# Four head groups and a memory attention: projections in another order, the gates of two groups in one product, 46 products ahead of the inverses

## The chip, the core and the metric

The kernel runs on one core of a Trainium2 chip. The metric is the device time of one execution in microseconds (us); the median of 3 runs of the kernel before is 945.6 us (944.08 to 947.56).

The engines are named as in the profile: PE (TensorE, the matrix engine; PEld is its weight load), DVE (VectorE), ACT (ScalarE), POOL (GpSimd) and SP (SyncE, which here only issues transfers). Each engine works through its own list of instructions in order and waits for others by semaphores.

## What is computed

One layer on `x` of 1024 tokens by 1024 features, in float32. All four head groups read one normalised input through one combined projection:

```python
h = rms_norm(x, pre_norm_g)
proj = h @ w_in + b_in      # columns: a_q a_k a_v a_i a_f a_z | b_x b_z | c_r c_k c_v c_w c_a c_z | d_q d_k d_v d_f d_z
h_a = mlstm_chunkwise(a_q, a_k, a_v, a_i, a_f)     # A: matrix memory in chunks, stabilised by a running maximum
h_b = multiscale_pool(b_x)                         # B: trailing means over 2, 4, 8, 16
h_c = rwkv7_time_mix(c_r, c_k, c_v, c_w, c_a)      # C: S = S(diag(w) - kk^T (a kk)) + v^T k, step by step
h_d = forgetting_attention(d_q, d_k, d_v, d_f)     # D: softmax(q k^T/8 + F_t - F_s), F = cumsum log sigmoid(d_f)
y = concat(h_a*silu(a_z), h_b*silu(b_z), h_c*silu(c_z), h_d*silu(d_z)) @ w_out
x = x + rms_norm(y, post_norm_g)
x = x + rms_norm(memory_cross_attention(rms_norm(x), mem), xattn_post_g)   # 256 memory tokens, 4 heads
```

Group C is computed in 16 chunks of 64 tokens. Each chunk and head has a 64x64 triangular system, whose inverse is put together from 32x32 blocks. Group D is FoX, group A the mLSTM.

## The kernel before

**Products in three parts.** A float32 product is made of three passes: each operand is split into a high and a low part (`h` and `l` of the input, `wh` and `wl` of the weights), and `mm3` (lines 136 to 139) issues high by high, low by high and high by low. `wload` (line 111) loads a weight piece (`wr`), rounds it to `wh` on ACT (L122) and takes the rest `wl` on POOL (L126), or on DVE (L124) late in the program.

**Fillers.** The projections aren't run as one block. They are generators in a list, `fillers`, and `fill(n)` draws n units from it. A unit is three matmuls of 512 columns, or six of about 260 columns. The order of PE's instructions is the order of the code. The other engines' instructions are put in order by a planner, which orders by readiness and priority, so that what the code writes late may come early.

**The stages**, with their times in the profiled execution:

- to 150 us: input norm, transposes, projections of C (`cproj`, `cnorm`).
- 150 to 208: four `cprep`, which prepare decay, gates and the chunk operands of C (line 518 on). Behind each stands `fill(15)`. Among these fillers is the product of D's values and gates, `vgemm(O_DV, 260, 8, dvd)`: 256 columns of values and 4 gate columns, 32 units.
- 208 to 223: the "gram" products of C (L575). Their results are masked on POOL (L585, 16 of 64x512) and stored by SP to a scratch tensor `dN` (L592).
- `cinv` (line 595) inverts the 32x32 blocks: it loads `dN` into `n` (L597), prepares an identity on POOL (L599, L600), and runs 62 dependent operations on DVE (L604 and L606 in turn). The result goes out to `dTn` (L609) and `dTt` (L608), and `tinv(0)` loads 32x32 blocks of it (L618). Its first products are PE's L630, the next L638. `fill(NI)` with `NI = 70` stands between `cinv` and L630. Its units come from `rgemm(O_DK)` and `vgemm(O_AV, 264)` (A's values with 8 gate columns). The norm products of D's keys stand among them (L822, L823: sums of squares by a matrix of ones, whose inputs DVE splits in L161).
- 297 to 420: the chain of C over its chunks (`cprop`, L679 to L711), with `rgemm(O_AK)` and `zgemm(O_CZ, 2)` as fillers. `zgemm(O_CZ)` makes C's gate path: 96 matmuls of 512 columns.
- 434 to 529: the mLSTM over 8 tiles. `mpre` loads `e` (L1048, from `cd`), adds a mask on DVE (L1049), takes the exponential (L1051) and multiplies by the scores `ml` (L1055 on PE, L1057 on DVE). `mlstm` ends with a norm whose root is taken on POOL as a power (L143, L144), and `post()` scales by it (`hh`, L1087 on DVE, L1088 on POOL). The fillers around a tile are `G0, G1, GA, GB, GC = 14, 7, 2, 4, 4` (before the first, before the second, and three per tile), from `bgemm`, `zgemm(O_BZ)` and `zgemm(O_AZ)`. `post()` of tile i runs in tile i+1, that of the last behind the loop.
- from 538: FoX. `Fp` holds F per head and key, in two halves (`t<-fd`, L1196 loads), and POOL adds the causal mask to it (L1206, 8 of 128x256 for each half). Each step has PE's scores (L1254, L1255), DVE's sum (L1256), ACT's exponential (L1262, tile `lg`) and PE's transposes (L1272).
- to the end: output projection, memory attention.

Of the kernel before, what the change touches and what calls it, by code (L numbers as in the profile page):

```python
# [11 lines left out]
ALU = mybir.AluOpType  # L12
# [14 lines left out]
O_BX, O_BZ = 1032, 1288  # L27
# [4 lines left out]
def bcast(ap, n):  # L32
    return bass.AP(tensor=ap.tensor, offset=ap.offset, ap=[[0, 128], [1, n]])
# [3 lines left out]
def tile_trunk(ctx: ExitStack, tc: tile.TileContext, a, out, dbg=None):  # L37
# [73 lines left out]
    def wload(src, scale=None):  # L111
        shape = [src.shape[0], src.shape[1], src.shape[2]] if len(src.shape) == 3 else [src.shape[0], src.shape[1]]
        with tc.high_priority():
            raw = wtile("wr", shape)
            SY.dma_start(raw, src)
            hi, lo = wtile("wh", shape), wtile("wl", shape)
            if scale is not None:
                for x, c in enumerate(scale):
                    SC.activation(hi[:, x, :], raw[:, x, :], AF.Copy, scale=c)
                    V.scalar_tensor_tensor(lo[:, x, :], raw[:, x, :], c, f32(hi[:, x, :]), op0=ALU.mult, op1=ALU.subtract)  # L120
                return hi, lo
            SC.copy(hi, raw)  # L122
            if cur["wp0"] is not None:
                V.tensor_tensor(lo, raw, f32(hi), op=ALU.subtract)  # L124
            else:
                G.tensor_tensor(lo, raw, f32(hi), op=ALU.subtract)  # L126
        return hi, lo
# [13 lines left out]
    def rstd_pow(tag, ss, n, eps, w=1):  # L141
        r = base(tag, [128, w])
        G.tensor_scalar(r, ss, 1.0 / n, eps, op0=ALU.mult, op1=ALU.add)  # L143
        G.tensor_tensor(r, r, mhalf[:, 0:w], op=ALU.pow)  # L144
        return r

    def norm_rows(src, gbc, dst):
        r = base("tn", [128, 1])
        SC.activation(dst, src, AF.Square, accum_out=r)
        r = rstd_pow("tn", r, D, EPS)  # L150
        V.scalar_tensor_tensor(dst, src, r, gbc, op0=ALU.mult, op1=ALU.mult)

    def gload(pool, tag, ap):
# [84 lines left out]
    def xnorm(i):  # L238
        x_t = xp("x", [128, 1024])
        SY.dma_start(x_t, a["x"][0, i * 128:(i + 1) * 128, :])  # L240
        xn = xp("xn", [128, 1024])
        r = base("tn", [128, 1])
        SC.activation(xn, x_t, AF.Square, accum_out=r)
        r = rstd_pow("tn", r, D, EPS)
        V.tensor_scalar(xn, x_t, r, None, op0=ALU.mult)
        xn_.append(xn)

# [346 lines left out]

    def cinv():
        Nt = cc("n4", [128, 32, 32])
        SY.dma_start(Nt, dN)  # L597
        Tn = cc("n4", [128, 32, 32])
        G.memset(Tn, 0.0)  # L599
        G.memset(Tn.rearrange("p a b -> p (a b)")[:, ::33], 1.0)  # L600
        for j in range(31):
            m = 31 - j
            pr = cc("pr", [128, m, j + 1])
            V.tensor_tensor(pr, Nt[:, j, j + 1:32][:, :, None].to_broadcast([128, m, j + 1]),  # L604
                            Tn[:, j, 0:j + 1][:, None, :].to_broadcast([128, m, j + 1]), op=ALU.mult)
            V.tensor_tensor(Tn[:, j + 1:32, 0:j + 1], Tn[:, j + 1:32, 0:j + 1], pr, op=ALU.add)  # L606
        V.tensor_copy(Nt, Tn.rearrange("p a b -> p b a"))
        SY.dma_start(dTt, Nt)  # L608
        SY.dma_start(dTn, Tn)  # L609
# [45 lines left out]
            SC.copy(SV[c - 1][0:64, 1::2, :], p[0:64, :, 64:128])  # L655

    FA, FB, FC = 2, 2, 2
    NI = 70
    BN = {}

    def cbk(c):
# [81 lines left out]
            SY.dma_start(yu[i * 128:(i + 1) * 128, 1, :], yc)  # L743


    def vgemm(c0, n, gc0, dst):
        ng = n - 256
        b = cm("bias", [128, 264])
        SY.dma_start(b[:, 0:n], bcast(b_in[c0:c0 + n], n))

        zz = []

        def ev(i, p):
            if i % 2 == 0:
                zz.append(cur["stg"]("zu", [128, 2, 256]))
            z, g = zz[-1][:, i % 2, :], gates[:, i, gc0:gc0 + ng]
            SC.copy(z, p[:, 0:256])
            SC.copy(g, p[:, 256:n])  # L758
            if i % 2:
                V.tensor_tensor(zz[-1], zz[-1], b[:, None, 0:256].to_broadcast([128, 2, 256]), op=ALU.add)  # L760
                g = gates[:, i - 1:i + 1, gc0:gc0 + ng]
                V.tensor_tensor(g, g, b[:, None, 256:n].to_broadcast([128, 2, ng]), op=ALU.add)
                SY.dma_start(dst[(i - 1) * 128:(i + 1) * 128, :].rearrange("(a p) c -> p a c", a=2), zz[-1])
        yield from ngemm_q(w_in, c0, n, hact, ev)

    def zgemm(c0, g, halves=False):
        def ev1(c, hf, p):
# [183 lines left out]
    with tc.manual_schedule(engines={PE}):  # L951
        run(cproj(6, 1))
        run(cproj(2, 2))
        fillers += [cproj(0, 2), cproj(4, 2), vgemm(O_DV, 260, 8, dvd), rgemm(O_DQ, 66, 0, 46, (7, 5, 5, 5))]
        gs = [cnorm(hf, j) for hf in range(2) for j in range(2)]
        for g in gs:
            next(g)
# [8 lines left out]
        for n, g in enumerate(gs):  # L966
            with tc.issue_after(act["cnorm"].ins):
                next(g)
            if g is gs[-1]:
                act["ln"] = tc.keep_in_program_order(SC.preload_act_table_set("natural_log_exp_and_others"))  # L970
            fill(15)
            if n:
                run(gs[n - 1])
        fill(4)
        run(gs[-1])
        c1.close()
        fillers += [rgemm(O_DK, 68, 256, 47, (6, 6, 5, 5)), vgemm(O_AV, 264, 0, avd), rgemm(O_AQ, 0, 512)]
# [25 lines left out]
        for c in range(16):  # L1003
            cchain(c)
            if c < 3:
                next(ti[1], None)
            if c >= 3:
                next(gr, None)
            if c >= 9:
                next(ac, None)  # L1010
        run(ac)
        cstore()
# [47 lines left out]
    def mlstm(i, vt, e):  # L1060
# [6 lines left out]
        if i > 0:  # L1067
# [6 lines left out]
        dn = base("tm", [128, 4])  # L1074
# [7 lines left out]
        ss = base("tm", [128, 4])  # L1082
        V.tensor_reduce(ss, h4(sq), AX.X, ALU.add)
        r = rstd_pow("tm", ss, 64, EPS, 4)

        def post():
            V.tensor_tensor(h4(hh), h4(hh), bc4(r), op=ALU.mult)  # L1087
# [71 lines left out]
            V.tensor_tensor(hi[r2], raw[r2], f32(hi[r2]), op=ALU.subtract)  # L1159
            qst[h] = hi  # L1160

    fillers += [bgemm(), zgemm(O_BZ, 1), zgemm(O_AZ, 0)]
    G0, G1, GA, GB, GC = 14, 7, 2, 4, 4
    bp = [bpool(0), bpool(1)]
    with tc.manual_schedule(engines={PE}):
        fill(G0)
        pre = mpre(0)
        fill(G1)
        post = None
        for i in range(NT):  # L1170
# [29 lines left out]
    am.close()  # L1200
    db = Pool("db", {"v": 2, "lg": 2, "pt": 3, "rE": 1})
    V.tensor_scalar(maskD, maskD, -NEG, None, op0=ALU.mult)
    for i in range(NT):
        for j in range(2):
            t = Fp[j][:, :, i * 128:(i + 1) * 128]
            G.tensor_tensor(t, t, maskD[:, None, :].to_broadcast([128, 2, 128]), op=ALU.add)  # L1206
# [330 lines left out]
    for g in range(1, 3):  # L1537
# [51 lines left out]
```

## Time and profile before

| | |
|---|---|
| median of 3 runs | 945.6 us (944.08 to 947.56) |
| profiled execution | 945.55 us |
| its span on the core | 943.7 us |
| PE busy | 895.3 us, 6041 matmuls |
| DVE, ACT, POOL busy | 544.3, 440.0, 223.2 us |
| mean granted clock of PE | 0.988 |

The profiled execution is the one from which all durations come; it lies at the median of the runs. The span is 1.85 us shorter than the time of the same execution. In a row of the timeline the columns are start (us), duration (us), engine, line, operation, output<-inputs, shape, count, and in brackets the idle time of the engine just before with what ended it. A matmul's duration overlaps that of the next, so its price is the distance from one start to the next. PEclk is the granted clock as a share of full speed.

### The profile page before, as it was taken

How to read it: one execution, taken by the hardware profiler on the slowest of the kernel's cores; microseconds unless marked ns; L12 is line 12 of the kernel's file. 1: busy time of each engine (PE TensorE's matmuls, PEld its weight loads, DVE VectorE, ACT ScalarE, POOL GpSimd, SP SyncE). 2: the span in 40 equal slices, each digit the busy share in tenths (PEclk: the TensorE clock that was granted, in tenths of full speed). 3: DMA queues.
4: the chain of work that ended last, by engine and by line, in shares of the span. 5: the costliest groups of instructions: out<-in, count | busy, mean ns of one | idle time of the engine just before them, and what ended most of it. 6: DMA issues, size and time to landing. Idle time of an engine off the chain costs nothing. (4 is left out here: it accounts for less than half of the span.)

```text
span 943.7 us, 16237 instructions
## 1 busy us (share of the span) xinstructions
PE 895.3 (95%) x6041; PEld 757.4 (80%) x6041; DVE 544.3 (58%) x1265; ACT 440.0 (47%) x1009; POOL 223.2 (24%) x244
## 2 busy tenths in 40 slices
PE   6999999999799999998998979999999999999997
PEld 6988887887598777776776667888887888889997
DVE  7684046973873347662698547656675455554225
ACT  7587156545455345642443335444454343444221
POOL 1002221139212243533334622000000000121211
PEclk9999999999999999999999989999999999999999
DMA  8977211132244122316465667533245311153104
GB/s 281 287 226 247 80 45 46 34 85 35 90 139 110 39 87 78 124 46 157 119 172 150 212 204 227 175 93 101 79 146 205 96 34 35 34 177 111 38 1 179
DMA packets 94431, 113.86 MB, mean 121 GB/s; under 512 B 21072, under 2 KB 68752, under 8 KB 94352
## 3 DMA queue, kind: packets, MB, share of 16 engines
q1 hardware_dynamic: 94208, 112.71, 38.9%
q8 instruction: 48, 0.79, 0.3%
q14 instruction: 31, 0.25, 0.1%
q10 hardware_dynamic: 144, 0.11, 0.1%
HBM read 83.92 MB, written 28.87 MB: 120 GB/s over the span
## 5 line engine op out<-in xcount | busy, mean ns | idle before, releaser
L137 PE MATMUL mm<-h,wh 128*128 128x512 f32 x528 | 221.3, 419 | 0.3 <-ACT zu L773 0.3
L138 PE MATMUL mm<-l,wh 128*128 128x512 f32 x528 | 210.4, 399 | 0.0
L139 PE MATMUL mm<-h,wl 128*128 128x512 f32 x528 | 210.3, 398 | 0.0
L126 POOL TENSOR_TENSOR wl<-wr,wh 128x512 fp32r<-128x512 f32 (+2 forms) x74 | 101.6, 1375 | 372.6 <-ACT wh L122 356.4
L137 PEld LDWEIGHTS mm<-h,wh 128*128 128x128 f32 x528 | 101.2, 192 | 24.0 <-issue 1.1
L139 PEld LDWEIGHTS mm<-h,wl 128*128 128x128 f32 x528 | 101.0, 191 | 23.4
L138 PEld LDWEIGHTS mm<-l,wh 128*128 128x128 f32 x528 | 101.5, 192 | 17.3 <-issue 0.2
L122 ACT CAST wh<-wr 128x512 fp32r<-128x512 f32 (+2 forms) x122 | 74.6, 620 | 71.6 <-PE mm L138 32.5
L137 PE MATMUL mm<-wh,act 128*128 128x256 f32 x256 | 72.7, 284 | 0.0
L138 PE MATMUL mm<-wl,act 128*128 128x256 f32 x256 | 71.9, 281 | 0.0
L139 PE MATMUL mm<-wh,act 128*128 128x256 f32 x256 | 71.8, 281 | 0.0
L137 PE MATMUL mm<-h,act 128*128 128x512 f32 x128 | 53.6, 419 | 0.9 <-DVE zu L771 0.4
L139 PE MATMUL mm<-h,act 128*128 128x512 f32 x128 | 50.5, 394 | 0.0
L138 PE MATMUL mm<-l,act 128*128 128x512 f32 x128 | 50.2, 392 | 0.0
L137 PEld LDWEIGHTS mm<-wh,act 128*128 128x128 f32 x256 | 48.3, 189 | 0.1
L138 PEld LDWEIGHTS mm<-wl,act 128*128 128x128 f32 x256 | 48.3, 188 | 0.0
L139 PEld LDWEIGHTS mm<-wh,act 128*128 128x128 f32 x256 | 48.2, 188 | 0.0
L137 PE MATMUL mm<-mT,wh 128*128 128x256 f32 x128 | 37.3, 291 | 8.9 <-ACT wh L122 8.9
L137 PE MATMUL mm<-wh,h 128*128 128x260 f32 (+1 forms) x128 | 37.4, 292 | 2.5 <-ACT gates L758 1.6
L1519 DVE TENSOR_TENSOR o<-mm,gb 128x256 f32<-128x256 f32 x32 | 13.6, 424 | 43.8 <-ACT junk L1518 43.6
L1465 ACT ACTIVATE e<-lgp,tf,r 128x256 f32<-128x256 f32 x32 | 18.0, 564 | 43.2 <-DVE tf L1462 43.2
L139 PE MATMUL mm<-mT,wl 128*128 128x256 f32 x128 | 37.0, 289 | 0.3 <-DVE wl L124 0.3
(408 smaller groups left out, 1996.0 us busy)
## 6 DMA issues: line engine op xcount, KB each, us to landing
wr<-in_w_in_dram SPq DMA_DIRECT2D x50, 256.0 KB, 2.9
wr<-in_wkv_dram SPq DMA_DIRECT2D x32, 256.0 KB, 3.9
x<-in_x_dram SPq DMA_DIRECT2D x16, 512.0 KB, 5.1
x<-x1d SPq DMA_DIRECT2D x15, 512.0 KB, 5.7
wr<-in_xattn_wo_dram SPq DMA_DIRECT2D x16, 256.0 KB, 3.0
vwd<-row SPq DMA_DIRECT2D x8, 512.0 KB, 4.0
rT<-zu SPq DMA_DIRECT2D x16, 256.0 KB, 2.1
zT<-zu SPq DMA_DIRECT2D x16, 256.0 KB, 3.1
```

What stands on the lines that cost most here:

```text
L122: SC.copy(hi, raw)
L126: G.tensor_tensor(lo, raw, f32(hi), op=ALU.subtract)
L137: T.matmul(o, lh, rh, start=st, stop=False, skip_group_check=skip)
L138: T.matmul(o, lh, rl, start=False, stop=False, skip_group_check=skip)
L139: T.matmul(o, ll, rh, start=False, stop=sp, skip_group_check=skip)
L1465: SC.activation(e, p, AF.Exp, bias=nb, scale=r2[:, i:i + 1], accum_out=dn)
L1519: V.tensor_tensor(o3[i][:, gs], p, xog[:, gs], op=ALU.mult)
```

## The change

It moves projections and waits; the number of PE's matmuls stays the same.

- D's values leave the fillers of the `cprep` stage, without the gate columns (256 wide), and take the place of `zgemm(O_CZ)` in the chain of C. `zgemm(O_CZ)` goes behind the fillers of the mLSTM, where `G0, G1, GA, GB, GC` become 18, 9, 3, 5, 5.
- The four gate columns of D join A's values in one product of 268 columns, from an array `w_av` packed on the host. The gates of both groups are then copied at once.
- `fill(15)` becomes `fill(13)`, four times; `NI` goes from 70 to 46.
- The load of `dN` in `cinv` is issued by ACT and not by SP. A flag `vsplit` sends the low parts of weights from POOL to DVE between the last `cprep` and `cinv`.
- `post()` of the last mLSTM tile goes into the loop, ahead of its `fill(GC)`. In FoX the masks are written in `fmask(i)`, called one tile ahead. The convolution of A is drawn from chunk 8 on, not 9, and small tiles share one tag.

```diff
-            SY.dma_start(Nt, dN)       # cinv
+            SC.dma_start(Nt, dN)
...
-            if cur["wp0"] is not None:
+            if cur["wp0"] is not None or cur.get("vsplit"):
                 V.tensor_tensor(lo, raw, f32(hi), op=ALU.subtract)
...
-    NI = 70
+    NI = 46
...
-    def vgemm(c0, n, gc0, dst):
+    def vgemm(wd, bias, c0, n, dst):
...
-            z, g = zz[-1][:, i % 2, :], gates[:, i, gc0:gc0 + ng]
+            z = zz[-1][:, i % 2, :]
             SC.copy(z, p[:, 0:256])
-            SC.copy(g, p[:, 256:n])
+            if ng:
+                SC.copy(gates[:, i, :], p[:, 256:n])
...
-        fillers += [cproj(0, 2), cproj(4, 2), vgemm(O_DV, 260, 8, dvd), rgemm(O_DQ, 66, 0, 46, (7, 5, 5, 5))]
+        fillers += [cproj(0, 2), cproj(4, 2), rgemm(O_DQ, 66, 0, 46, (7, 6, 6, 6))]
...
-            fill(15)
+            fill(13)
             if n:
                 run(gs[n - 1])
+        cur["vsplit"] = True
         fill(4)
...
-        fillers += [rgemm(O_DK, 68, 256, 47, (6, 6, 5, 5)), vgemm(O_AV, 264, 0, avd), rgemm(O_AQ, 0, 512)]
+        fillers += [rgemm(O_DK, 68, 256, 47, (6, 6, 5, 5)), vgemm(a["w_av"], a["b_av"][0], 0, 268, avd), rgemm(O_AQ, 0, 512)]
...
         next(ti[0])
+        cur["vsplit"] = False
         fill(NI)
...
-        fillers += [rgemm(O_AK, 2, 768), zgemm(O_CZ, 2)]
+        fillers += [rgemm(O_AK, 2, 768), vgemm(w_in, b_in, O_DV, 256, dvd)]
...
-    fillers += [bgemm(), zgemm(O_BZ, 1), zgemm(O_AZ, 0)]
-    G0, G1, GA, GB, GC = 14, 7, 2, 4, 4
+    fillers += [bgemm(), zgemm(O_BZ, 1), zgemm(O_AZ, 0), zgemm(O_CZ, 2)]
+    G0, G1, GA, GB, GC = 18, 9, 3, 5, 5
...
             post = mlstm(i, *pre)
+            if i == NT - 1:
+                post()
             fill(GC)
...
-        post()
         next(bp[1])
...
-    for i in range(NT):
+    def fmask(i):
         for j in range(2):
             t = Fp[j][:, :, i * 128:(i + 1) * 128]
             G.tensor_tensor(t, t, maskD[:, None, :].to_broadcast([128, 2, 128]), op=ALU.add)
+
+    fmask(0)
...
+            if h == 1 and i < NT - 1:
+                fmask(i + 1)
```

Three places show what becomes of the order on the engines. Numbers at the names are those of the buffers; lines from 658 on are shifted by 2 to 8 in the kernel after.

The first is the load of `dN` ahead of the inverses. Before, it is the last of these rows on SP, behind a weight load `wr` that can only start when its buffer is free:

```order
L592 DMA dN<-bq_2296 32x8x32 x6
L592 DMA dN<-bq_2387 32x8x32 x8
L115 DMA wr_2827<-in_w_in_dram 128x2x256
L597 DMA n_439_2472<-dN 128x1024
L115 DMA wr_2879<-in_w_in_dram 128x2x264
L115 DMA wr_2897<-in_w_in_dram 128x2x264
```

After, it stands on ACT, between two steps of the norm of D's keys (`sm`, `zt`):

```order
L122 CAST wh_2623<-wr_2621 128x536
L828 ACTIVATE sm_2440<-sm_2440,epst 128x512
L809 ACTIVATE zt_2488<-zu_2195 128x512
L829 ACTIVATE sm_2440<-sm_2440 128x512
L597 DMA n_436_2326<-dN 128x1024
L160 CAST bv_2490<-zt_2488 128x256
```

The load has left the queue of weight loads; what POOL does ahead of the identity (L599) has not changed but for one low part.

The second is the start of the mLSTM on DVE (`e`: the tile of exponents, `q`: the low part of a convolved tile). Before, the product of the first tile stands behind the first mask:

```order
L1049 TENSOR_TENSOR e_4874<-e_4874,maskA 128x512
L1057 SCALAR_TENSOR_TENSOR e_4874<-ml_4881,e_4874 128x2x128
L1057 SCALAR_TENSOR_TENSOR e_4874<-ml_4882,e_4874 128x2x128
L1049 TENSOR_TENSOR e_4917<-e_4917,maskA 128x512
L1049 TENSOR_TENSOR e_5007<-e_5007,maskA 128x512
L1159 TENSOR_TENSOR q_5003<-u_5000,q_5003 64x1024
```

After, three masks stand ahead of it:

```order
L1053 TENSOR_TENSOR e_4732<-e_4732,maskA 128x512
L1053 TENSOR_TENSOR e_4781<-e_4781,maskA 128x512
L1053 TENSOR_TENSOR e_4890<-e_4890,maskA 128x512
L1061 SCALAR_TENSOR_TENSOR e_4732<-ml_4739,e_4732 128x2x128
L1061 SCALAR_TENSOR_TENSOR e_4732<-ml_4740,e_4732 128x2x128
L1061 SCALAR_TENSOR_TENSOR e_4781<-ml_4788,e_4781 128x2x128
```

The first product now needs the loads of three tiles of `e`, not of one.

The third is the start of FoX on POOL (`t`: the two halves of `Fp`; `tm` and `tc`: the root of the last mLSTM tile). Before:

```order
L126 TENSOR_TENSOR wl_5926<-wr_5923,wh_5925 128x512
L1206 TENSOR_TENSOR t_5808<-t_5808,maskD 128x2x128 x8
L126 TENSOR_TENSOR wl_5953<-wr_5950,wh_5952 128x512
L1206 TENSOR_TENSOR t_5811<-t_5811,maskD 128x2x128 x8
L143 TENSOR_SCALAR tm_5731<-tm_5729 128x4
L144 TENSOR_TENSOR tm_5731<-tm_5731,mhalf 128x4
L1088 TENSOR_TENSOR hh_5725<-hh_5725,na_g 128x256
```

After:

```order
L1212 TENSOR_TENSOR t_5796<-t_5796,maskD 128x2x128 x8
L126 TENSOR_TENSOR wl_5900<-wr_5897,wh_5899 128x512
L143 TENSOR_SCALAR tc_5707<-tc_5705 128x4
L144 TENSOR_TENSOR tc_5707<-tc_5707,mhalf 128x4
L1092 TENSOR_TENSOR hh_5701<-hh_5701,na_g 128x256
L1212 TENSOR_TENSOR t_5799<-t_5799,maskD 128x2x128 x8
L126 TENSOR_TENSOR wl_5927<-wr_5924,wh_5926 128x512
```

All eight masks of a half still stand together, and the power of the last mLSTM tile has gone ahead of the second half's.

More of the change, by code (lines that the diff above doesn't have):

```diff
@@ L68, in tile_trunk @@
     cur = {"wp0": None}
-    base = Pool("base", {"tn": 8, "tc": 8, "tf": 16, "tm": 8, "tt": 20})
+    base = Pool("base", {"tc": 8, "tf": 16, "tt": 20})
     c2 = Pool("c2", {})
@@ L147, in norm_rows @@
     def norm_rows(src, gbc, dst):
-        r = base("tn", [128, 1])
+        r = base("tc", [128, 1])
         SC.activation(dst, src, AF.Square, accum_out=r)
-        r = rstd_pow("tn", r, D, EPS)
+        r = rstd_pow("tc", r, D, EPS)
         V.scalar_tensor_tensor(dst, src, r, gbc, op0=ALU.mult, op1=ALU.mult)
@@ L241, in xnorm @@
         xn = xp("xn", [128, 1024])
-        r = base("tn", [128, 1])
+        r = base("tc", [128, 1])
         SC.activation(xn, x_t, AF.Square, accum_out=r)
-        r = rstd_pow("tn", r, D, EPS)
+        r = rstd_pow("tc", r, D, EPS)
         V.tensor_scalar(xn, x_t, r, None, op0=ALU.mult)
@@ L743, in cstore @@
             SY.dma_start(yu[i * 128:(i + 1) * 128, 1, :], yc)
-    def vgemm(c0, n, gc0, dst):
+    def vgemm(wd, bias, c0, n, dst):
         ng = n - 256
-        b = cm("bias", [128, 264])
-        SY.dma_start(b[:, 0:n], bcast(b_in[c0:c0 + n], n))
+        b = cm("bias", [128, 268])
+        SY.dma_start(b[:, 0:n], bcast(bias[c0:c0 + n], n))
         zz = []
@@ L755, in ev @@
                 zz.append(cur["stg"]("zu", [128, 2, 256]))
-            z, g = zz[-1][:, i % 2, :], gates[:, i, gc0:gc0 + ng]
+            z = zz[-1][:, i % 2, :]
             SC.copy(z, p[:, 0:256])
-            SC.copy(g, p[:, 256:n])
+            if ng:
+                SC.copy(gates[:, i, :], p[:, 256:n])
             if i % 2:
                 V.tensor_tensor(zz[-1], zz[-1], b[:, None, 0:256].to_broadcast([128, 2, 256]), op=ALU.add)
-                g = gates[:, i - 1:i + 1, gc0:gc0 + ng]
-                V.tensor_tensor(g, g, b[:, None, 256:n].to_broadcast([128, 2, ng]), op=ALU.add)
+                if ng:
+                    g = gates[:, i - 1:i + 1, :]
+                    V.tensor_tensor(g, g, b[:, None, 256:n].to_broadcast([128, 2, ng]), op=ALU.add)
                 SY.dma_start(dst[(i - 1) * 128:(i + 1) * 128, :].rearrange("(a p) c -> p a c", a=2), zz[-1])
-        yield from ngemm_q(w_in, c0, n, hact, ev)
+        yield from ngemm_q(wd, c0, n, hact, ev)
     def zgemm(c0, g, halves=False):
@@ L1008, in tile_trunk @@
                 next(gr, None)
-            if c >= 9:
+            if c >= 8:
                 next(ac, None)
@@ L1073, in mlstm @@
                 V.scalar_tensor_tensor(nu[:, h, :], pi[h % 2][:, h // 2, :], gk(2, i, h), nu[:, h, :], op0=ALU.mult, op1=ALU.add)
-        dn = base("tm", [128, 4])
+        dn = base("tc", [128, 4])
         SC.activation(dn, nu[:, :, 64], AF.Abs)
@@ L1081, in mlstm @@
         SC.activation(sq, hh, AF.Square)
-        ss = base("tm", [128, 4])
+        ss = base("tc", [128, 4])
         V.tensor_reduce(ss, h4(sq), AX.X, ALU.add)
-        r = rstd_pow("tm", ss, 64, EPS, 4)
+        r = rstd_pow("tc", ss, 64, EPS, 4)
         def post():
@@ L1545, in tile_trunk @@
     base.close()
-_INS = ["x", "memT", "post_norm_g", "w_in", "b_in", "norm_a_g", "decay_w2", "iclr_a2", "gn_c_g", "gn_c_b",
+_INS = ["x", "memT", "w_av", "b_av", "post_norm_g", "w_in", "b_in", "norm_a_g", "decay_w2", "iclr_a2", "gn_c_g", "gn_c_b",
         "w_out", "xattn_post_g", "xattn_wq", "wkv", "xattn_wo", "cols", "poolbd"]
@@ L1566, in _pack, with pick @@
         pw[r0:r0 + 64, g // 2, r0:r0 + 64] = w[g]
+    def pick(w):
+        w = np.asarray(w)
+        return np.concatenate([w[:, O_AV:O_AZ], w[:, O_DF:O_DZ]], axis=1)
     mt = np.asarray(a["mem"][0]).T.reshape(8, 128, 256).transpose(1, 0, 2)
     wkv = np.asarray(a["xattn_wkv"][0]).reshape(8, 128, 8, 256).transpose(1, 2, 0, 3)
-    return {"cols": np.concatenate([np.eye(128, dtype=cols.dtype), cols], axis=1), "poolbd": pw, "memT": mt, "wkv": wkv}
+    return {"cols": np.concatenate([np.eye(128, dtype=cols.dtype), cols], axis=1), "poolbd": pw, "memT": mt, "wkv": wkv, "w_av": pick(a["w_in"][0]), "b_av": pick(a["b_in"])}
 def kernel(**inputs):
```

## The prediction

> **What bounds the kernel now.** I read the page first, then PE's busy time by stretches, PE's waits, and last the timelines of the engines that PE waits for.
>
> ```profile
> span 943.7 us, 16237 instructions
> PE 895.3 (95%) x6041; PEld 757.4 (80%) x6041; DVE 544.3 (58%) x1265; ACT 440.0 (47%) x1009; POOL 223.2 (24%) x244
> ```
>
> PE is the bound: it is idle for 943.7 - 895.3 = 48.4 us in all. The change keeps the number of matmuls (widths 260 and 264 become 256 and 268), so PE's work stays. What it can win or lose is idle time and time at a lower clock. So I ask where these lie (columns: the stretch, its length, PE's busy time, granted clock, DMA share, GB/s).
>
> ```profile
> 223.50:286.92 63.42, 56.15 (x302) 0.97 0.33 96
> 434.50:529.20 94.70, 85.78 (x493) 0.95 0.59 156
> 538.00:553.00 15.00, 8.58 (x31) 0.77 0.40 142
> 600.00:705.00 105.00, 105.00 (x725) 1.00 0.35 109
> ```
>
> Idle are 7.27 us in the inverse stage, 8.92 in the mLSTM and 6.42 at the start of FoX; from 600 to 705 PE never waits. These three places hold 22.6 of the 48.4 us. A matmul of 512 columns also goes slower after a wait:
>
> ```profile
> 251.57 0.38 PE L823 MATMUL sm<-ysb,onesr 128*128 128x256 f32 x1 [3.61 <-DVE ysb L161]
> ...
> 252.57 0.63 PE L137 MATMUL mm<-h,wh 128*128 128x512 f32 x1
> 253.00 0.63 PE L138 MATMUL mm<-l,wh 128*128 128x512 f32 x1
> ...
> 255.88 0.39 PE L139 MATMUL mm<-h,wl 128*128 128x512 f32 x1
> 256.10 0.39 PE L137 MATMUL mm<-h,wh 128*128 128x512 f32 x1
> ```
>
> From start to start it is 0.43 us at 252.57 and 0.22 at 255.88: the seven slow ones cost about 1.5 us. The granted clocks give the same sort of loss: (1 - 0.95) of 85.78 = 4.3 us in the mLSTM, and in the FoX window 0.23 of 8.58 = 2.0 us.
>
> **The change part by part.**
>
> *D's values out of the first stage.* The move is 32 units. Their price comes from nine like products in a row, the first and the last of them:
>
> ```profile
> 285.73 0.28 PE L137 MATMUL mm<-wh,h 128*128 128x264 f32 x1
> ...
> 286.71 0.28 PE L139 MATMUL mm<-wh,l 128*128 128x264 f32 x1
> 286.92 2.11 PE L630 MATMUL sm<-t,bq 32*32 32x32 f32 x64
> ```
>
> Eight steps in 0.98 us are 0.122 each, so 192 matmuls are 23.4 us (units of 0.73). Eight units leave the `cprep` stage (4 times 15 to 13, 5.8 us) and 24 leave the fill to L630 (70 to 46; 17.2 us at 0.70 to 0.73 a unit). In the chain 22.4 us of D's values stand for 22.4 us of C's gate path (96 matmuls at 0.22 to 0.24), which costs nothing as long as the chain stays full; only one wait of 1.8 us (`cs` on `w`, quoted below) is there now, and an added one of that sort is my bound. The joined gates change no column count: 260 + 264 = 256 + 268.
>
> What the 32 units covered is the question. In `cprep`, PE waits 1.1 us for `gc`:
>
> ```profile
> PE cs L693 <- DVE w L681: 1.8, 1, 1.8
> PE sm L137 <- ACT gc L530: 1.1, 1, 1.1
> PE mm L137 <- DVE v L485: 0.8, 1, 0.8
> ```
>
> `gc` is one buffer, freed by DVE's work on the `cprep` before. With two units (1.4 us) less between two `cprep`, PE comes earlier to the same wait: 1.1 + 1.4 = 2.5 us, and another one may open. The 0.8 us for `v` goes with the reorder. I take +1.0 us (0 to +3).
>
> *The inverses.* L630 does not wait before (the row above has no bracket). What it needs is the end of this path:
>
> ```profile
> 208.07 1.52 PE L575 MATMUL sm<-t,bk 64*128 64x128 f32 x16
> 210.86 2.61 POOL L585 TENSOR_TENSOR t<-t,maskG 64x512 f32<-64x512 f32 x2 [4.70 <-ACT t L584]
> ...
> 236.46 0.16 POOL L600 MEMSET n<- 128x32 f32 x1
> 234.96 0.39 SPq L115 DMA_DIRECT2D wr<-in_w_in_dram  x1
> 235.67 0.34 SPq L597 DMA_DIRECT2D n<-dN  x1
> 239.35 0.54 DVE L604 TENSOR_TENSOR pr<-n,n 128x31 f32<-128x31 f32 x1 [14.42 <-DMA n<-dN]
> ...
> 246.59 1.48 DVE L606 TENSOR_TENSOR n<-n,pr 128x220 f32<-128x220 f32 x1
> 248.10 0.40 DVE L604 TENSOR_TENSOR pr<-n,n 128x231 f32<-128x231 f32 x1
> ...
> 256.06 0.42 DVE L161 TENSOR_TENSOR w<-zt,yc 128x256 fp32r<-128x256 f32 x1
> 256.39 0.42 DVE L606 TENSOR_TENSOR n<-n,pr 128x252 f32<-128x252 f32 x1
> 256.72 0.74 DVE L828 SCALAR_TENSOR_TENSOR zu<-zu,pc,sm 128x512 f32<-128x512 f32 x1
> 257.38 0.41 DVE L604 TENSOR_TENSOR pr<-n,n 128x247 f32<-128x247 f32 x1
> ...
> 271.47 0.32 SPq L609 DMA_DIRECT2D dTn<-n  x1
> ...
> 274.18 1.00 SPq L618 DMA_DIRECT2D t<-dTn  x2
> ```
>
> The gram products start at 208.07; POOL's 16 masks begin at 210.86, with a weight part and the identity behind them; SP issued the `dN` load at 235.67, 0.71 us after the weight load `wr` that stood ahead of it, which waits for a buffer that POOL's split frees. It landed at 239.35. The chain ended at 271.47 (32.1 us), the result came back by 274.18 plus about 3.5, so L630 could have gone at 277.7 and had 9.2 us to spare.
>
> After: gram starts at 208.1 - 5.8 + 1.0 = 203.3. The load on ACT no longer stands behind `wr` and would land about 228, but the identity (L600) still stands behind POOL's 16 masks: it ended 236.62 - 208.1 = 28.5 us behind the first gram product, so at 231.8 now. That, and no longer the load, starts the chain; the win is 239.35 - 236.62 = 2.7 us. The chain itself: four L606 next to a POOL split took 1.5 and not 0.4 us (246.59), some 4.6 us; eight L161 (0.33 each, 256.06 to 256.39) and four L828 (0.66) stand among its 62 operations, 5.3 us; pure it is 22. After, the order puts ten L161, six norm steps and four bias additions (3.3 + 4.0 + 1.7, the additions by the nearest rows at 0.33 to 0.66; 9.0 us) into it, and three POOL splits overlap it (3.3 us): 34.3 us. It ends at 266.1, and L630 can go 6.2 us later, at 272.3.
>
> PE without waits would take 78.8 us from the first gram product to L630 before, less 7.27 idle and 1.5 slow, less 17.2 for 24 units: 52.8, so it stands there at 256.1. It is then 272.3 - 256.1 = 16.2 us short, where it was idle and slow for 8.8. With 2 us slow behind the wait the loss is 16.2 + 2 - 8.8 = 9.4. The idle is partly at the norm products (their L161 stand in DVE's queue among the chain), mostly at L630. Bounds: the nearest row for a shorter chain is the pure 22 us (12 less, so no loss but a gain of 3), for a longer one five splits and not three, or the load behind ACT's norm steps (+3). I take +9.4, and for the range +4 to +13.
>
> The Trainium skill, "TensorE: Matmul & The Clock Gate", Part 1, states that the clock halves after an idle window of about 3.4 us and needs as long a busy one to come back, in a window that runs freely. The slow row behind a wait of 3.61 us agrees; the mLSTM's granted clock of 0.95, with no wait over 2.8 us, is more than a bare limit of 3.4 us would give. By the page alone the waits in the mLSTM would cost no clock and the win below would be 4 us smaller.
>
> *The mLSTM.* Its waits are these, and DVE's before the first tile:
>
> ```profile
> PE ml L1093 <- DVE e L1057: 2.8, 1, 2.8
> PE ml L1100 <- DVE ks L1096: 1.8, 1, 1.8
> PE ml L1055 <- DVE e L1057: 1.6, 1, 1.6
> 440.00 0.69 DVE L1049 TENSOR_TENSOR e<-e,maskA 128x512 f32<-128x512 f32 x1 [10.97 <-DMA e<-cd]
> ...
> 447.19 0.69 DVE L1049 TENSOR_TENSOR e<-e,maskA 128x512 f32<-128x512 f32 x1 [1.87 <-DMA e<-cd]
> ```
>
> There are 13 units per tile in place of 10 (2.1 us more cover each), and 4 and 2 more ahead of the first two tiles (2.8 and 1.4 us). That covers 1.8 and 1.6 and most of 2.8. Against it stands the new order on DVE: the first product needs the third tile's load of `e`, which lands 7 us behind the first today; with the cover this is 0 to 2.7 us of wait. I leave 2.7 us of waits and 1.1 slow: 3.8, of 8.92 + 4.3 = 13.2, so the win is 9.4 (4 to 12).
>
> *The start of FoX.*
>
> ```profile
> 538.98 5.52 POOL L1206 TENSOR_TENSOR t<-t,maskD 128x256 f32<-128x256 f32 x8 [3.29 <-DMA t<-fd]
> 544.87 1.02 POOL L144 TENSOR_TENSOR tm<-tm,mhalf 128x4 f32<-128x4 f32 x1
> 545.91 0.43 DVE L1087 TENSOR_TENSOR hh<-hh,tm 128x256 f32<-128x256 f32 x1 [7.62 <-POOL tm L144]
> 547.38 0.48 PE L1272 MATMUL tr<-cst,lg 128*128 128x128 f32 x1 [6.42 <-ACT lg L1262]
> ```
>
> The second half's masks on POOL hold up the power of the last tile, that holds DVE at `hh`, and FoX's first sum stands behind it in DVE's queue. After, the power has gone ahead of these masks, and five units (3.5 us) stand behind `post()`. So the 6.42 us go, with the 2.0 slow. A weight part now stands behind the second masks on POOL; PE may wait for it, about 1 us (0 to 5.5, if the whole mask batch is exposed). The win is 7.4 (2 to 8.4). The other edits (shared tags, convolution from chunk 8, `gates` copied once) move work of engines that are 58% busy or less. They cost nothing under PE's full stretches; bare, one of them is worth one short wait, as the 1.8 us of `cs`.
>
> **The sum**: +1.0 +9.4 -9.4 -7.4 = -6.4. From 945.55 us (the profiled execution, which lies on the median of 945.6) this gives 939 us.
>
> **The rivals.**
>
> R1, the stall at the inverses stays small. For it: SP's `wr` is gone from ahead of the load, and if DVE's insertions fall where it waits anyway, the chain is nearer 28 than 34 us. Then the loss is 9.4 - 6.3 = 3.1, the sum -12.7, the time 933; with both gains at their upper bounds (12 and 8.4) it is 929.
>
> R2, nothing is won: the mLSTM's waits are DVE's and not PE's lack of work. For it speaks the new order of three masks ahead of the first product; if DVE falls behind by one load (2.7 us) and keeps half its waits, the win there is 4, the sum -1, the time 944.5. This includes that the mask edit doesn't do what its words say: the order on POOL still has eight masks together. Where that batch is fully exposed, FoX wins 2 and the time is 945.55 + 1.0 + 9.4 - 9.4 - 2 = 944.5, too.
>
> R3, slower. One mechanism: `cinv` starves PE. Before, 9.2 us of filler are to spare at L630; after, none, so each us by which the chain ends later than 266.1 is a us of PE. From 6.4 us later (272.5) all gains are eaten. With five splits of POOL over the chain and not three (+2.2), the `dN` load held on ACT behind norm steps that themselves wait for PE and DVE (+3), and a DVE that waits in the chain for products which PE issues late (two waits of 3.6 us, as at 251.57), the chain ends 12.4 later: 945.55 - 6.4 + 12.4 = 951.5 us. Against it: before, none of the insertions made DVE wait inside the chain, and fewer splits stand ahead of POOL's identity.
>
> **How the numbers follow.** My forecast (939, own range 934 to 943) has 0.40, R1 0.30, R2 0.18, R3 0.12. A change under 0.5%, 4.7 us, is about what a measurement of this kernel can't tell from none. Faster than 940.9 are R1 and three quarters of the forecast: 0.30 + 0.30 = 0.60. The rest of the forecast, R2 and the nearer part of R3 lie within: 0.10 + 0.18 + 0.02 = 0.30. Slower than 950.3 is the rest of R3, 0.10. The range goes from R1's better end, 929, to just short of R3, 948.
>
> **What would show it.** In the changed kernel's profile: gram starts near 203, DVE's L604 near 232 with idle ahead that ends with POOL's identity or the load; L630 with a bracket of about 10 us and near 272; between 223 and 272 PE's granted clock below 0.97. In the mLSTM, PE idle 3 us, not 8.9, and granted 0.98 or more. At FoX no bracket over 2 us at the first `tr`. In the chain no new wait. The forecast is wrong if L630 goes before 266 or after 278, or if the mLSTM still idles 7 us.

## The result, and the profile after

The kernel after takes 952.4 us (median of 4 runs, 950.8 to 954.6), the kernel before 945.6 (4 runs). The ratio is 1.0072, 95% interval 1.0044 to 1.0100: slower by 0.7%, where 939 us were forecast. The profiled execution took 950.8 us with a span of 949.0; it is the fastest of the four, so what follows accounts for 5.3 of the 6.7 us between the medians.

The page of the kernel after:

```profile
span 949.0 us, 16228 instructions
PE 901.5 (95%) x6041; PEld 763.1 (80%) x6041; DVE 543.8 (57%) x1262; ACT 440.6 (46%) x1001; POOL 221.5 (23%) x243
PEclk9999999899959999999999999999999999999999
```

PE issues the same 6041 matmuls and is idle for 47.5 us, where it was 48.4. So the idle time hardly moved in sum. But PE is busy for 6.2 us longer: part of its work ran at the lower clock, which the twelfth slice shows (0.5, 261 to 285 us). To find where, I take the first matmul of each stage on PE's timeline, in both kernels, and subtract the work that the change moved: the projection matmuls counted in each stage, at the distance from start to start that is usual in full stretches (0.231 us for 512 columns, 0.118 to 0.124 for 256 to 268). Up to the gram products 192 of 260 columns are gone and 72 of 512 have come; up to L638 72 of 512 columns are gone, since the units that leave at the end of that fill are wide ones:

| stage | before | after | work moved | lost (+) or won (-) | forecast |
|---|---|---|---|---|---|
| to the first gram product | 208.1 | 203.9 | -6.4 | +2.2 | +1.0 |
| to the first L638 | 84.5 | 79.9 | -16.3 | +11.7 | +9.4 |
| to the mLSTM's first scores | 141.9 | 144.7 | +3.3 | -0.5 | 0 |
| to FoX's first scores | 104.5 | 113.6 | +19.4 | -10.3 | -9.4 |
| FoX, to the transposes of the memory attention | 175.8 | 178.2 | 0 | +2.4 | -7.4 |
| to the end | 228.9 | 228.7 | 0 | -0.2 | 0 |

The last column adds to -6.4, the one before it to 5.3, which is the difference of the spans. FoX carries most of the error, 9.8 us, and the inverses 2.3. Stages differ from run to run, too: one that no edit touches can be 2.4 us longer in one profile than in another (the chain in experiments 5 and 8 below), so single rows of that size say little.

The stretches of the kernel after (stretch, length, PE busy, granted clock, DMA share, GB/s), from the end of the gram products, from L630, the mLSTM, and the start of FoX:

```profile
219.75:274.76 55.01, 41.80 (x231) 0.86 0.32 101
274.76:290.00 15.24, 15.00 (x187) 0.73 0.32 65
428.50:542.10 113.60, 110.17 (x611) 1.00 0.55 154
542.10:575.00 32.90, 23.77 (x105) 0.92 0.66 215
```

The mLSTM did what was forecast: 3.4 us idle in place of 8.92, at a full clock. The inverse stage is idle for 13.2 us, and FoX's first 33 us have 9.1 us of idle time. PE's waits name them (each line: us in total, how often, the longest):

```profile
PE sm L630 <- DMA t<-dTn: 7.0, 1, 7.0
PE mm L137 <- ACT zu L775: 3.8, 1, 3.8
PE mm L137 <- ACT gates L759: 3.8, 2, 3.0
PE tr L1303 <- DVE zt L1244: 3.7, 1, 3.7
PE sm L137 <- ACT gc L530: 2.6, 1, 2.6
PE sm L825 <- DVE ysb L161: 2.4, 1, 2.4
PE mm L139 <- POOL wl L126: 1.2, 1, 1.2
```

L630 now waits for the inverse (7.0), with 6.2 us at three other places of that stage (`gates` twice, `ysb` once). The 6.4 us of FoX's first transposes are gone, and in their place stand 3.8 for `zu`, 3.7 for `zt` and 1.2 for a weight part.

How the inverse came late, on the timeline of the kernel after:

```profile
233.51 0.19 DVE L604 TENSOR_TENSOR pr<-n,n 128x31 f32<-128x31 f32 x1 [4.19 <-POOL n L600]
...
266.51 1.08 DVE L607 COPY n<-n 128x1024 f32<-128x1024 f32 x1
...
266.59 0.38 SPq L609 DMA_DIRECT2D dTn<-n  x1
269.88 0.38 SPq L115 DMA_DIRECT2D wr<-in_w_in_dram  x1
...
270.86 1.49 SPq L618 DMA_DIRECT2D t<-dTn  x2
...
267.38 0.43 PE L139 MATMUL mm<-wh,l 128*128 128x268 f32 x1
274.76 3.40 PE L630 MATMUL sm<-t,bq 32*32 32x32 f32 x64 [6.95 <-DMA t<-dTn]
278.10 0.59 PE L137 MATMUL mm<-wh,h 128*128 128x268 f32 x1
278.48 0.43 PE L138 MATMUL mm<-wl,h 128*128 128x268 f32 x1
278.71 0.43 PE L139 MATMUL mm<-wh,l 128*128 128x268 f32 x1
```

The chain starts with POOL's identity (forecast 231.8, measured 233.5), takes 33.0 us (forecast 34.3), and its result is back 8.3 us later (forecast 6.2): SP stands at a weight load (269.88) between the store and the loads. L630 goes at 274.76, forecast was 272.3. The clock cost more than I allowed: L630's 64 small matmuls take 3.40 us, not 2.11 as before, and those behind it stand 0.22 us apart, not 0.12, until about 283. These are 1.3 and some 2.2 us; the 18 ahead of the wait stand 0.22 apart too and cost another 1.8. Together with the idle time, 13.2 where it was 7.3, that is 11.2 of the 11.7 us.

How FoX's start lost what it had won, on the same kernel's timeline:

```profile
541.58 6.04 POOL L1212 TENSOR_TENSOR t<-t,maskD 128x256 f32<-128x256 f32 x8 [4.95 <-DMA t<-fd]
547.58 1.26 POOL L126 TENSOR_TENSOR wl<-wr,wh 128x512 fp32r<-128x512 f32 x1
...
537.98 0.45 SPq L1145 DMA_DIRECT2D ybT<-u  x1
548.87 0.33 SPq L1317 DMA_DIRECT2D wr<-in_w_out_dram  x1
...
551.98 0.62 ACT L1319 CAST h<-wr 128x512 fp32r<-128x512 f32 x1 [7.21 <-DMA wr<-in_w_out_dram]
...
555.60 0.52 PE L137 MATMUL mm<-h,wh 128*128 128x512 f32 x1 [3.83 <-ACT zu L775]
...
572.63 0.41 PE L1303 MATMUL tr<-cst,rE 128*128 128x128 f32 x2 [3.73 <-DVE zt L1244]
```

The weight part `wl` stands on POOL behind the second batch of eight masks. SP's next load of `w_out` (548.87) can start only then, and SP had issued nothing since 537.98. SP's own list of waits says so in the kernel after (first line below). Before, SP stood still for nearly as long, but at the store of the last tile's `hh`, which stood behind the same masks (the two lines after it):

```profile
SPq L1317 <- POOL wl L126: 17.3, 2, 10.4
SPq L1089 <- POOL hh L1088: 24.4, 8, 8.8
547.24 0.32 SPq L1089 DMA_DIRECT2D yu<-hh  x1
```

In the kernel after, behind SP's load stand the loads of `dv`, of F's tiles and of all gates. ACT stands at the cast of that piece until 551.98, so it evicts `zu` late, and DVE's gates come late 17 us further on; how much of this last wait is the masks' experiment 1 shows. Before, PE was itself waiting (6.42 us) while SP stood still, and met only 0.3 and 0.5 us at the same two places.

### The profile page after: what moved, and what is told of

It is laid out like the page before. It is cut to its first block, busy times and chain, and to the rows that moved or that the text cites. A ratio compares the mean times of both kernels' runs of the same rounds, so it can differ in the third digit from the quotient of the medians.

```text
span 949.0 us, 16228 instructions
## 1 busy us (share of the span) xinstructions
PE 901.5 (95%) x6041; PEld 763.1 (80%) x6041; DVE 543.8 (57%) x1262; ACT 440.6 (46%) x1001; POOL 221.5 (23%) x243
## 5 line engine op out<-in xcount | busy, mean ns | idle before, releaser
L126 POOL TENSOR_TENSOR wl<-wr,wh 128x512 fp32r<-128x512 f32 (+1 forms) x73 | 99.9, 1370 | 368.1 <-ACT wh L122 343.1
L122 ACT CAST wh<-wr 128x512 fp32r<-128x512 f32 (+1 forms) x122 | 74.4, 620 | 82.4 <-PE mm L138 38.5
L137 PE MATMUL mm<-wh,h 128*128 128x268 f32 (+1 forms) x128 | 40.2, 314 | 3.8 <-ACT gates L759 3.8
L138 PE MATMUL mm<-wl,h 128*128 128x268 f32 (+1 forms) x128 | 37.9, 296 | 0.0
```

The source lines that it names most:

```text
L137: T.matmul(o, lh, rh, start=st, stop=False, skip_group_check=skip)
L138: T.matmul(o, lh, rl, start=False, stop=False, skip_group_check=skip)
```

## The experiments

Ratios are to the kernel before, run on the same chip with each set; 3 rounds where nothing else is said. The kernel after has 1.0072 (1.0044 to 1.0100). Stage times come from one profiled run each; that of experiment 5 is the slowest of its ten, 3.2 us above their median. My theories were two. First, that FoX's new waits come from the masks, by way of SP. Second, that the inverse stage lacks the units that the mLSTM got, and that nothing is free in between. The rivals stand in each expectation.

### 1. Masks really one tile ahead

In the kernel after, all eight masks of a half stay together, as the order had shown: the planner moves them up as soon as their data are there. Here they are tied behind the last weight part.

```diff
-                G.tensor_tensor(lo, raw, f32(hi), op=ALU.subtract)
+                act["wl"] = G.tensor_tensor(lo, raw, f32(hi), op=ALU.subtract)
...
-            G.tensor_tensor(t, t, maskD...)
+            with tc.issue_after(act["wl"].ins):
+                G.tensor_tensor(t, t, maskD...)
...
-    fmask(0)
+    fmask(0, (0,))          # the second half's first mask: behind ftr(0)
```

> The kernel after, with the FoX masks really one tile ahead: on POOL only the first tile's mask of each half stands ahead of the weight parts, the other fourteen behind the last of them. Theory A (the start of FoX moved its stall: SP stands at a load of w_out until POOL has split a weight piece behind the second batch of eight masks, 548.87 us in the kernel after, so the w_out pieces, ACT's casts and DVE's gate come late): the first weight part goes about 5 us earlier, SP's block ends near 539, the PE waits of 1.2, 3.8 and 3.7 us between 548 and 573 shrink to under 3 in all with about 1 us less at the lower clock; total 5 to 9 us below the kernel after, about 945. Rival B (these waits come from the bandwidth of the loads or from ACT's own queue, not from the masks): the waits stay, total within 2 us of the kernel after, 951 to 953.

Measured: 942.3 us, ratio 0.9982 (0.9964 to 0.9999): 0.9% below the kernel after. FoX takes 169.6 us, not 178.2. On the timeline of this run:

```profile
538.82 0.74 POOL L1213 TENSOR_TENSOR t<-t,maskD 128x256 f32<-128x256 f32 x1 [2.05 <-PE ml L1143]
539.52 1.75 POOL L126 TENSOR_TENSOR wl<-wr,wh 128x512 fp32r<-128x512 f32 x1
541.22 11.61 POOL L1213 TENSOR_TENSOR t<-t,maskD 128x256 f32<-128x256 f32 x14
...
541.29 0.33 SPq L1318 DMA_DIRECT2D wr<-in_w_out_dram  x1
```

The weight part is done at 541.27 and not at 548.84, and SP's load follows it in both kernels by 0.02 to 0.03 us. PE's waits in that stretch fall to 0.3 and 2.0. Theory A holds for the load, for `zu` and for the total. For `zt` it is shown only in part: that wait is 2.0 here, but 3.7, 3.9 and 3.0 in experiments 5, 8 and 10, which have the same late masks. In experiment 5 DVE's gates stand behind the low parts of `w_out` pieces, and these behind ACT's casts, which wait for the loads of the pieces; so at this place the rival may hold. On the timeline of experiment 5:

```profile
562.53 0.62 ACT L1334 CAST h<-wr 128x512 fp32r<-128x512 f32 x1 [1.76 <-DMA wr<-in_w_out_dram]
563.18 0.69 DVE L1335 TENSOR_TENSOR l<-wr,h 128x512 fp32r<-128x512 f32 x1 [2.65 <-ACT h L1334]
```

### 2. The identity ahead of the gram masks

```diff
+        Tid = cident()          # the two memsets of cinv, first
         cgram(0, 1)
         cgram(1, 1)
-        cinv()
+        cinv(Tid)
```

> The kernel after, with the identity for the inverses set on POOL ahead of the gram products' masks and not behind them. Theory A (POOL's identity starts the chain of 62 DVE operations, not the load of dN): the chain starts when the load lands, near 229.5 and not at 233.5, PE's wait at the first product of tinv falls from 6.95 to about 3 us, total 4 us lower (948), a little more if the clock stays up. Rival B (the operations inserted into DVE's queue wait for PE and ACT and set the chain's end): the chain starts earlier but ends under 1.5 us earlier, total within 1.5 us of the kernel after.

Measured: 948.9 us, ratio 1.0058 (1.0041 to 1.0075), its interval overlaps that of the kernel after. The start on this run's timeline, and the wait in its list of waits:

```profile
230.97 1.34 DVE L607 TENSOR_TENSOR pr<-n,n 128x31 f32<-128x31 f32 x1
232.34 1.24 DVE L609 TENSOR_TENSOR n<-n,pr 128x31 f32<-128x31 f32 x1
```

```profile
PE sm L633 <- DMA t<-dTn: 6.9, 1, 6.9
```

Counted from the first gram product, the chain starts at 25.3 us and not at 29.6, as theory A has it, but ends only 2.3 us earlier: its first two operations now lie beside POOL's last gram mask and a weight split and take 1.34 and 1.24 us, not 0.19 and 0.21, and the wait at the inverse's first product stays (PE itself comes earlier, since a norm product ahead waits 1.2 us and not 2.4). Half of theory A, half of its rival; as a change of the total it can't be told from nothing.

### 3 and 4. The units back at the inverses, or all of D's values back in the first stage

```diff
-    NI = 46                      # experiment 3
+    NI = 70
```

```diff
-        fillers += [cproj(0, 2), cproj(4, 2), rgemm(O_DQ, 66, 0, 46, (7, 6, 6, 6))]      # experiment 4, and NI = 70
+        fillers += [cproj(0, 2), cproj(4, 2), vgemm(w_in, b_in, O_DV, 256, dvd), rgemm(O_DQ, 66, 0, 46, (7, 5, 5, 5))]
-            fill(13)
+            fill(15)
-        fillers += [rgemm(O_AK, 2, 768), vgemm(w_in, b_in, O_DV, 256, dvd)]
+        fillers += [rgemm(O_AK, 2, 768)]
```

> The kernel after with 70 units and not 46 ahead of the inverse's products; the 24 units then lack in the chain of C (17 us of PE work). Theory A (the chain has slack: PE is busy there only because the fillers are there): no wait at the first product of tinv, about 10 us won there, nothing lost in the chain; total about 942. Rival B (the chain's own latency needs these units): idle time appears in the chain, up to 17 us, and the total is 952 to 959. The chance of A is about even, since PE is never idle from 300 to 440 us in the kernel after and the trace does not show the chain's slack.

> The kernel after with D's values back in the first stage (256 wide, gates still joined with A's), 15 units behind each cprep and 70 ahead of the inverse's products as before; C's gate path stays in the mLSTM, so the chain of C has 32 units (22.4 us) fewer. Theory A (the loss lies in the first stage alone and the chain has slack): the stage up to the inverses takes the time of before, the mLSTM keeps its win of 10.5, total about 938. Rival B (the chain needs the units): idle time of up to 22 us in the chain, total 945 to 960.

Measured: 954.4 us, ratio 1.0102 (1.0080 to 1.0124), and 950.9 us, ratio 1.0068 (1.0048 to 1.0087). The chain's stretch of PE in the kernel after, then in experiment 3, then in experiment 4:

```profile
289.20:428.50 139.30, 139.28 (x1325) 0.99 0.30 88
```

```profile
295.90:430.40 134.50, 127.84 (x1238) 0.94 0.27 79
```

```profile
298.00:427.00 129.00, 122.39 (x1136) 0.92 0.25 77
```

The inverse stage wins what was expected: in both runs L630 goes without a wait, and from the gram products to L638 they take 85.9 and 83.7 us, before 84.5. But the chain, full in the kernel after, now idles for 6.6 us in each, at a granted clock of 0.94 and 0.92. From L638 to the mLSTM's scores it is shorter by 5.0 us for 24 units (16.9 us) fewer, and by 10.7 for 32 units (22.4) fewer: 11.9 and 11.7 us are lost. Rival B holds: the chain had little slack. The 32 units for the mLSTM are paid for at the inverses or in the chain, at about the 10.3 us that they win. Not all of the inverse stage hangs on the number of units: the 3.8 us at `gates` stay in experiment 3 and fall to 1.6, as before, in experiment 4. Nor were the load of `dN` on ACT, `vsplit` and the joined gates run by themselves, so their shares stay open.

### 5 and 8. Half of C's gate path

On the version with late masks, 16 units of C's gate path go back to the chain and `NI` is 62; experiment 8 has the identity first as well.

```diff
-    NI = 46
+    NI = 62
...
-        fillers += [rgemm(O_AK, 2, 768), vgemm(w_in, b_in, O_DV, 256, dvd)]
+        fillers += [rgemm(O_AK, 2, 768), vgemm(w_in, b_in, O_DV, 256, dvd), zhalf(O_CZ, 2, 0)]
-    fillers += [bgemm(), zgemm(O_BZ, 1), zgemm(O_AZ, 0), zgemm(O_CZ, 2)]
-    G0, G1, GA, GB, GC = 18, 9, 3, 5, 5
+    fillers += [bgemm(), zgemm(O_BZ, 1), zgemm(O_AZ, 0), zhalf(O_CZ, 2, 1)]
+    G0, G1, GA, GB, GC = 16, 8, 3, 4, 4
```

> The kernel after with the late masks of the first experiment, and C's gate path cut in two: 16 units of it back in the chain of C, 16 in the mLSTM (its fillers 16, 8, 3, 4, 4), and 62 units, not 46, ahead of the inverse's products, so that the chain keeps the number of its units. Theory A (the loss at the inverses and the win in the mLSTM are two ends of one trade, with the last units of each end worth least in the mLSTM): the wait of 7 us at the first product of tinv goes, and some 4 us at the lower clock with it; the mLSTM gives back 2 to 4 us; total 5 to 8 us below the run with late masks alone, ratio to before 0.990 to 0.993. Rival B (the mLSTM needs all 32 units): it gives back 10 us, ratio 0.998.

> The version with C's gate path cut in two and 62 units ahead of the inverses, plus the identity ahead of the gram masks on POOL. Theory A (with 62 units PE no longer waits for the chain's end, so an earlier end is worth nothing but the wait at a norm product, 2 us): 0 to 2 us below the version without. Rival B (the chain's end still sets L630): 3 us or more below it.

Measured: 941.5 us, ratio 0.9977 (0.9954 to 1.0000), and 937.0 us, ratio 0.9927 (0.9900 to 0.9954). In the lists of waits of 5 and of 8:

```profile
PE sm L638 <- DMA n<-dTt: 4.3, 1, 4.3
```

```profile
PE sm L641 <- DMA n<-dTt: 4.1, 1, 4.1
```

The wait at L630 is gone in both, but half-way through L638 PE waits for the transposed result, whose loads stand on SP between weight loads. In experiment 5 the stretch from L638 to the mLSTM's scores takes 151.8 us, 7.1 more than in the kernel after for 1.8 us of work less: 8.9 are lost there, 4.3 of them this wait. So experiment 5 won nothing over late masks alone, against theory A, though not as its rival has it: the mLSTM gave back only about 1 us (104.8 us with 14 units fewer behind its first scores). Experiment 8 is better than 5 by 0.5% as the medians go, but the intervals touch at 0.9954. Its stage from the gram products to L638 is 2.0 us shorter, which is theory A. The total is lower by more, as the rival's number has it, but the rival's mechanism is not there, since L630 waits in neither run: the rest of the difference lies in later stages that the edit doesn't touch, and how much of it is the identity's stays open.

### 6. The FoX part alone on the kernel before

```diff
             post = mlstm(i, *pre)
+            if i == NT - 1:
+                post()
             fill(GC)
...
+            with tc.issue_after(act["wl"].ins), tc.issue_after(act["hh"].ins):   # behind the last POOL step of post(), too
                 G.tensor_tensor(t, t, maskD...)
```

> The kernel before with the FoX part alone: post() of the last mLSTM tile in the loop, and the masks behind that tile's power and the last weight parts on POOL. Theory A (POOL's second batch of masks ahead of that power is what stalls the start of FoX): PE's wait of 6.4 us and 2 us at the lower clock go, total 6 to 8 us below before, ratio 0.992 to 0.994. Rival B (the stall moves on, to the loads of w_out, as it did in the kernel after): waits of 3 to 4 us appear within the next 30 us, ratio 0.997 to 1.003.

Measured: 937.9 us, ratio 0.9934 (0.9909 to 0.9958). FoX takes 169.9 us, before 175.8. This run's first 35 us of FoX, and what is left of the wait:

```profile
539.50:575.00 35.50, 30.73 (x154) 1.00 0.74 243
```

```profile
PE tr L1276 <- ACT lg L1266: 2.4, 2, 1.3
```

Theory A holds. The FoX win that I forecast is there to be had (5.9 of 7.4 us), if the masks really move.

### 7. PE kept busy during the wait

```diff
         fill(NI)
+        pdum = ps("cw", [128, 512])
+        for x in range(22):
+            T.matmul(pdum, hact(0, 0)[0], hslice(0, 0, 512)[0], start=True, stop=True)
```

> The kernel after with late masks, and 22 matmuls of 512 columns (6 to 7 us, result unused) where PE waits for the first product of tinv, so that PE is busy during that wait. They add no useful work and delay nothing if they fit. Theory A (after the wait PE runs at half clock, which costs about 4 us from 264 to 281): the 64 small matmuls take 2.1 us and not 3.4, the 268-column ones behind them 0.12 and not 0.22, total 2 to 4 us below the run with late masks alone. Rival B (the slow matmuls come from something else, such as weight loads or PSUM): total the same or up to 2 us more.

Measured: 943.0 us, ratio 0.9988 (0.9967 to 1.0009), the same as late masks alone. On its timeline, and the granted clock from 275 to 280:

```profile
266.80 5.89 PE L1000 MATMUL cw<-h 128*128 128x512 f32 x22
273.96 2.61 PE L630 MATMUL sm<-t,bq 32*32 32x32 f32 x64 [1.27 <-DMA t<-dTn]
276.51 0.59 PE L137 MATMUL mm<-wh,h 128*128 128x268 f32 x1
276.90 0.43 PE L138 MATMUL mm<-wl,h 128*128 128x268 f32 x1
```

```profile
275.00:280.00 5.00, 5.00 (x53) 0.51 0.28 44
```

Under the 22 matmuls the granted clock rose from 0.50 to 1.00 (270.0 to 272.7), and after a wait of 1.27 us and the 64 small matmuls it was at half again. L630 won 0.8 us, the matmuls behind it nothing. Theory A's win did not come, and the rival has the total right; but its causes are not shown, since the slow matmuls go with a granted clock of 0.51. So the size of the clock's part stays open: it could not be taken away separately.

### 9 and 10. Two versions that beat both kernels (5 rounds)

Experiment 9 is the FoX part alone plus half of C's gate path moved to the mLSTM. Experiment 10 is experiment 8 with the transposed result on ACT's queue.

```diff
-        fillers += [rgemm(O_AK, 2, 768), zgemm(O_CZ, 2)]                     # experiment 9, on 6
+        fillers += [rgemm(O_AK, 2, 768), zhalf(O_CZ, 2, 0)]
-    fillers += [bgemm(), zgemm(O_BZ, 1), zgemm(O_AZ, 0)]
+    fillers += [bgemm(), zgemm(O_BZ, 1), zgemm(O_AZ, 0), zhalf(O_CZ, 2, 1)]
-    G0, G1, GA, GB, GC = 14, 7, 2, 4, 4
+    G0, G1, GA, GB, GC = 16, 8, 3, 4, 4
```

```diff
-        SY.dma_start(dTt, Nt)                                                # experiment 10, on 8
+        SC.dma_start(dTt, Nt)
...
-            SY.dma_start(tt[b0:b0 + 32, :, 0:32], dTt...)                    # and the second one
+            (SC if hf == 0 else SY).dma_start(tt[b0:b0 + 32, :, 0:32], dTt...)
```

> The FoX part alone on the kernel before, plus one half of C's gate path (16 units, 11 us) moved from the chain of C to the mLSTM (its fillers 16, 8, 3, 4, 4); the first stage and the 70 units at the inverses stay as before. Theory A (the chain has some slack: without 32 units it lost 12 of 22 us, and the first units out cost least): the chain loses 3 to 5 us, the mLSTM wins 6 to 8, total 1 to 4 us below the FoX part alone, ratio to before 0.989 to 0.992. Rival B (a unit is worth the same in the chain and in the mLSTM): ratio 0.992 to 0.996.

> The best version so far (late masks, half of C's gate path moved, 62 units, early identity), with the inverse's transposed result stored to and loaded from dTt by ACT's queue and not by SP's. Theory A (SP stands at weight loads that wait for POOL's splits, and the loads from dTt, which PE waits for 4.1 us at L641, stand behind them): that wait goes, total 2 to 4 us below the version without, ratio 0.988 to 0.991. Rival B (ACT stands at these transfers itself and PE waits for its evictions): the wait comes back at another place, ratio 0.992 to 0.997.

Measured: 936.8 us, ratio 0.9925 (0.9896 to 0.9955), and 933.9 us, ratio 0.9922 (0.9901 to 0.9943). Two lines of waits, of 9 and of 10:

```profile
PE cs L699 <- DVE uu L695: 2.5, 2, 2.2
```

```profile
PE mm L137 <- ACT gates L762: 5.2, 3, 3.0
```

In 9 the chain starts to wait for DVE when its units run out; with 16 units fewer, less the two that `G0` draws ahead of the first scores, it is shorter by 3.2 us than in experiment 6, so 6.6 us are lost, which theory A put at 3 to 5. The mLSTM is 1.0 us longer for the 14 units (9.8 us) drawn there, so 8.8 are won, more than its 6 to 8. In 10 the wait of 4.1 us at the second product is gone and 1.4 us more stand at `gates`; from L638 to the scores it takes 144.2 us where experiment 8 took 149.4, from the gram products to L638 2.4 more. Both ratios lie just inside the rivals' ranges, but their intervals reach into those of both theories, so the totals decide neither. The versions 6, 8, 9 and 10 can't be told apart by their intervals; the lowest is 10, 0.8% below before.

## Why the prediction was wrong

The step that failed is "the start of FoX", and in it the sentence "A weight part now stands behind the second masks on POOL; PE may wait for it, about 1 us (0 to 5.5, if the whole mask batch is exposed)". The mechanism was seen and priced for PE alone: that wait is 1.2 us. What was left out is that SP's queue waits for the same weight part to free a buffer, and that the loads of `w_out`, the gates and D's values are queued behind. The first wait did go (6.42 us to nothing), and 8.8 us of waits stand in its place within 30 us. Experiment 1 shows it: with the masks out of the way FoX is 8.6 us shorter, though 2.0 us of the wait for `zt` stay. With that, the term is 169.6 - 175.8 = -6.2, against the -7.4 of the sum.

"Where that batch is fully exposed, FoX wins 2" was the rival that came nearest, but it counted one batch of masks and not the loads behind it. That the mask edit "doesn't do what its words say" was right, and should have weighed more.

"The inverses" had the right mechanism and was too small: +9.4 forecast, +11.7 measured. The chain's start, its length and L630 came within 2.5 us. Idle time was less than forecast (13.2 us, not 16.2), the loss by the clock more: 2 us were set down for it behind L630, and there the rows show 3.5, with 1.8 ahead of it. The result's way through memory was 2.1 us longer, by a weight load on SP. R3 named this place, but it did not need the late chain of R3 for a slower kernel: that chain ended at 266.5, as forecast, and that the 951.5 us of R3 lie near the measured time is chance.

The Trainium skill ("TensorE: Matmul & The Clock Gate", Part 1) ties the slow clock to an idle window of about 3.4 us that runs freely. Experiment 7 has no such pause: 1.27 us idle, then 64 matmuls of 32 rows and columns, and the granted clock from 275 to 280 is 0.51. So PE counted as busy in the profile was not enough there, and a bare limit of 3.4 us misses it; why, no run here shows.

"The mLSTM" (-9.4 forecast) measured -10.3, and the feared wait for the third tile's load of `e` did not come. "In the chain no new wait" held, with 0.5 us won. `cprep` lost 2.2, forecast 1.0; its wait for `gc` is 2.6 us, forecast 2.5. So nearly every sign that the prediction named came out, only the wait at L630 is 7.0 and not 10 us; none of them looks at FoX beyond its first transposes, where the error lay.

What the prediction did not ask is where the 32 units could have come from at no price. Experiments 3 and 4 answer: neither from the chain nor from the stages ahead of it. All 32 cost 11.7 us in the chain, or the 13.9 that the first two stages lose in the kernel after, and win 10.3 in the mLSTM; half of them, in experiment 9, cost 6.6 and win 8.8.

## What to carry to other kernels

When a step goes past another in an engine's queue, price the queues that wait for what it delays: a split that frees a buffer is awaited by the load queue, and with it by everything behind that load. A wait that goes is won only up to the next thing that is late; follow the transfers that were hidden behind it for as long as they were held, here to 30 us past the wait. And an edit that writes instructions later in the code moves nothing when a planner orders them by readiness; tie them to an instruction, and look at the order again.

## What the runs showed of the hardware

After a pause of 1.27 us and 64 matmuls of 32x32 PE's granted clock was half (0.51 from 275 to 280 us in experiment 7), while the same 64 matmuls with no wait just ahead took 2.11 us (before, at 286.92). Two DVE operations on 31 columns took 1.34 and 1.24 us beside a mask and a weight split on POOL (experiment 2), and 0.19 and 0.21 in the kernel after, where POOL ran short memsets at that time.
